# Layer normalisation without affine terms: the first tile loaded in halves and stored in parts, the last stores waited for on GpSimd

## The chip, the cores and the metric

The kernel runs on one core of a Trainium2 chip. The metric is the device time of one execution in microseconds (us). The profile is of one execution; its span reaches from the first to the last instruction of the program, and the device time is a little longer, since it takes in what lies around the program. The core has four engines that matter here: VectorE (DVE), ScalarE (ACT) and GpSimd (POOL) compute, SyncE (SP) only waits and starts transfers. Transfers between main memory (HBM) and on-chip memory run on 16 DMA engines, which take their work from queues; SP's transfers are on one queue (q1 in the profile), ACT's on another (q10).

## The reference

Each of the 32 x 512 = 16384 rows of 1024 floats is normalised on its own: its mean is taken off, and it is divided by the root of its variance plus eps.

```
def reference(x, eps):                     # x: (32, 512, 1024) float32
    mean = np.mean(x, axis=-1, keepdims=True)
    var = np.var(x, axis=-1, keepdims=True)
    return ((x - mean) / np.sqrt(var + eps)).astype(np.float32)
```

The input and the output are 67.11 MB each, so 134.2 MB have to be moved.

## The kernel before, in words

The 16384 rows are spread over the 128 partitions, which gives each partition 128 rows. They are cut into 17 tiles (line 10): 15 of 8 rows per partition, one of 6 and one of 2. A tile of 8 rows is 4096 KB; in main memory the rows of one partition lie side by side, so such a tile is moved as one contiguous run of 32 KB for each partition (`rows_of`, line 82).

On chip there is one buffer, `ring`, with room for 48 rows per partition, that is, for six tiles of 8 (lines 12 and 53). A tile is loaded into it, normalised in place and stored from it.

The order of the work is written out by hand; each engine has its own program, and they wait for each other through semaphores.

- SP issues all 17 loads (lines 93 to 104). The first six find room at once. Each later load waits until the stores of the tiles that had its rows before have landed (the semaphores `stored`, lines 100 and 104). So the load of tile 6 waits for the store of tile 0. `BESIDE` (line 16) could put loads on ACT's queue and is empty.
- DVE (`vector`, line 107) waits for a tile's load (`landed`), runs two `bn_stats` for each row, one for each half of the row's 1024 elements, and then a reciprocal, for which it waits for ACT's root.
- GpSimd (lines 145 to 190) merges the statistics of a tile in nine small operations, and makes the bias in a tenth, after the reciprocal.
- ACT (lines 193 to 213) takes the root for the tile, then normalises row after row with one ACTIVATE each (line 202), and issues the store of the whole tile (line 211), which waits until the tile's last row is done (`act`).
- At the end SP waits for the stores of the tiles that are still in the ring (lines 216 to 218). Then the engines meet in the program's closing: SP gives a signal (line 52 of the profile), each engine answers it, SP collects the answers, and GpSimd gathers all engines and clears the semaphores (line 249).

DVE's program for the middle tiles is a loop, which is why it compares with a value in a register there (lines 128 to 131). A DMA adds 16 to its semaphore when it has landed wholly, one for each DMA engine; `sixteens` (line 74) counts what a wait must reach.

Of the kernel before, what the change touches and what calls it, by code (L numbers as in the profile page):

```python
# [12 lines left out]

FIRST, TURNS = 3, 2

BESIDE = ()


@with_exitstack
def kernel(  # L20
# [6 lines left out]
    nc = tc.nc  # L27
# [3 lines left out]
    x2 = x.flatten_outer_dims()  # L31
    o2 = out.flatten_outer_dims()
# [10 lines left out]
    def sbuf(name, shape):  # L43
        return ctx.enter_context(nc.sbuf_tensor(name, shape, fdt))


    plan, row = [], 0
# [5 lines left out]
    ring = sbuf("ring", [P, SLOT * SLOTS, D])  # L53
# [13 lines left out]
    def places(name):  # L67
        out = [nc.alloc_semaphore(f"{name}_{t}") for t in range(FIRST + SLOTS)]
        for t in range(len(out), len(plan)):
            looped = t < FIRST + TURNS * SLOTS  # L70
            out.append(out[t - SLOTS] if looped else nc.alloc_semaphore(f"{name}_{t}"))
        return out

    def sixteens(sems, t):
        return 16 * sum(1 for s in sems[: t + 1] if s.num == sems[t].num)

    landed, rooted, stored = places("landed"), places("rooted"), places("stored")
    taken, inverse, pool, act = map(
        nc.alloc_semaphore, ("taken", "inverse", "pool", "act")
    )  # L80

    def rows_of(a, row, K):
        return a[row * P : (row + K) * P].rearrange("(p k) d -> p k d", p=P)

    def load(engine, t):
        K, row, at = plan[t]
        return engine.dma_start(  # L87
            out=ring[:, at : at + K, :], in_=rows_of(x2, row, K)
        ).then_inc(landed[t], 16)


    owner = {}
    for t, (K, row, at) in enumerate(plan):
        gone = sorted({owner[r] for r in range(at, at + K) if r in owner})
        owner.update((r, t) for r in range(at, at + K))
        if t in BESIDE:
            assert not gone
            load(nc.scalar, t)
            continue
        for g in gone[:-1]:  # L100
            nc.sync.wait_ge(stored[g], sixteens(stored, g))
        dma = load(nc.sync, t)
        if gone:
            dma._wait_ge(stored[gone[-1]], sixteens(stored, gone[-1]))


    def vector(t, arrived, turn):
        K, row, at = plan[t]
        for k in range(K):
            for s in range(NSUB):  # L110
                i = nc.vector.bn_stats(  # L111
                    out=stats[:, at + k, s, :],
                    in_=ring[:, at + k, s * BN_MAX : (s + 1) * BN_MAX],
                )
                if k == 0 and s == 0:
                    i._wait_ge(landed[t], arrived)
        i.then_inc(taken, 1)
        nc.vector.reciprocal(  # L118
            out=rstd[:, at : at + K], in_=std[:, at : at + K]
        )._wait_ge(rooted[t], turn).then_inc(inverse, 1)  # L120

    nc.vector.memset(eps_t[:], eps_val)  # L122
    for t in range(FIRST):
        vector(t, 16, 1)
# [3 lines left out]
    with nc.vector.Fori(16, 16 * TURNS + 1, 16) as arrived:  # L128
        for t in range(FIRST, FIRST + SLOTS):
            vector(t, nc.vector.lower_val(arrived), turn)  # L130
        nc.vector.reg_add(turn, turn, 1)
    for t in range(FIRST + TURNS * SLOTS, len(plan)):
        vector(t, 16, 1)
# [4 lines left out]
    def gp(i, sem, value):  # L138
        nonlocal npool
        i._wait_ge(sem, value).then_inc(pool, 1)  # L140
        npool += 1
        return pool, npool

    g = nc.gpsimd
    for t, (K, row, at) in enumerate(plan):
        parts = stats[:, at : at + K].rearrange("p g s (h c) -> p g (s h) c", h=2)
        mean4, m2 = parts[:, :, :, 1], parts[:, :, :, 2]
        nm, d, h = nmean[:, at : at + K], dev[:, :K], half[:, :K]
        n = gp(
            g.tensor_tensor(out=h, in0=mean4[:, :, 0:2], in1=mean4[:, :, 2:4], op=ALU.add),  # L150
            taken,
            t + 1,
        )
        n = gp(g.tensor_tensor(out=nm, in0=h[:, :, 0], in1=h[:, :, 1], op=ALU.add), *n)  # L154
        n = gp(
            g.tensor_scalar(out=nm, in0=nm, scalar1=-1.0 / H, scalar2=None, op0=ALU.mult),  # L156
            *n,
        )
        n = gp(
            g.tensor_tensor(  # L160
                out=d, in0=mean4, in1=nm.unsqueeze(2).to_broadcast([P, K, H]), op=ALU.add
            ),
            *n,
        )
        n = gp(g.tensor_mul(out=d, in0=d, in1=d), *n)  # L165
        n = gp(
            g.tensor_scalar(  # L167
                out=d, in0=d, scalar1=float(D // H), scalar2=None, op0=ALU.mult
            ),
            *n,  # L170
        )
        n = gp(g.tensor_tensor(out=d, in0=d, in1=m2, op=ALU.add), *n)  # L172
        n = gp(g.tensor_tensor(out=h, in0=d[:, :, 0:2], in1=d[:, :, 2:4], op=ALU.add), *n)  # L173
# [3 lines left out]
                    out=ss[:, at : at + K], in0=h[:, :, 0], in1=h[:, :, 1], op=ALU.add  # L177
# [7 lines left out]
                    out=nmr[:, at : at + K], in0=nm, in1=rstd[:, at : at + K]  # L185
# [7 lines left out]
    for t, (K, row, at) in enumerate(plan):  # L193
        nc.scalar.activation(  # L194
            out=std[:, at : at + K],
            in_=ss[:, at : at + K],
            func=AF.Sqrt,
            bias=eps_t[:],
            scale=1.0 / D,
        )._wait_ge(*summed[t]).then_inc(rooted[t], 1)  # L200
        for k in range(at, at + K):
            i = nc.scalar.activation(  # L202
                out=ring[:, k, :],
                in_=ring[:, k, :],
                func=AF.Identity,
                bias=nmr[:, k : k + 1],
                scale=rstd[:, k : k + 1],
            ).then_inc(act, 1)
            if k == at:
                i._wait_ge(*ready[t])  # L210
        nc.scalar.dma_start(
            out=rows_of(o2, row, K), in_=ring[:, at : at + K, :]
        )._wait_ge(act, row + K).then_inc(stored[t], 16)


    for t in range(len(plan)):
        if t in owner.values():
            nc.sync.wait_ge(stored[t], sixteens(stored, t))


# [33 lines left out]
```

## Time and profile before

| | us |
|---|---|
| time, median of 3 runs (lowest to highest) | 318.0 (317.92 to 318.02) |
| time of the profiled execution | 318.23 |
| its span | 316.6 |
| ACT: one row, line 202, mean of 128 | 1.227 |
| DVE: one half row, line 111, mean of 256 | 0.678 |
| load of 4096 KB, median from issue to landing | 43.9 |
| store of 4096 KB, median from issue to landing | 48.0 |
| first load, from issue to landing | 12.2 |

The time from issue to landing of a transfer holds the time that it waits behind others in its queue and shares the 16 DMA engines with the other queue; it isn't what the transfer would take alone. In the lines of the profile, a queue's instruction is marked by a q behind its engine's name (SPq, ACTq), and DMA shares and GB/s are means over the 16 DMA engines.

### The profile page before, as it was taken

The numbers are of one execution on the slowest core, as the hardware profiler recorded it, in microseconds if no ns is written. First come the engines' busy times: TensorE is split into PE (matmuls) and PEld (weight loads), VectorE is DVE, ScalarE is ACT, GpSimd is POOL, SyncE is SP. The second block draws the span as 40 slices with busy tenths as digits, with TensorE's granted clock in tenths as the row PEclk, the third lists the DMA queues.
The fourth block names the chain that finished last, engine by engine and source line by source line (L and its number), as shares of the span: only waits on it lengthen the run. The fifth ranks groups of instructions, "written<-read, shape, count | busy, mean of one in ns | idle before, by whom it ended". The sixth has DMA issues, their size and how long they took to land.

```text
span 316.6 us, 693 instructions
## 1 busy us (share of the span) xinstructions
DVE 156.8 (50%) x274; ACT 153.0 (48%) x146; POOL 39.3 (12%) x174
## 2 busy tenths in 40 slices
DVE  0387595875290743809347092561916519083000
ACT  1006595775915619074290833808347092567500
POOL 0002202112002020010201102020020200203100
DMA  8999999999999999999999999999999999999995
GB/s 331 397 464 402 426 431 397 461 402 460 423 440 439 422 451 410 455 410 451 410 460 414 447 418 435 418 443 431 439 443 418 447 418 435 431 431 422 455 421 254
DMA packets 4899, 134.24 MB, mean 424 GB/s; under 512 B 544, under 2 KB 544, under 8 KB 544
## 3 DMA queue, kind: packets, MB, share of 16 engines
q1 hardware_dynamic: 2448, 67.11, 49.6%
q10 hardware_dynamic: 2448, 67.11, 49.1%
q14 instruction: 3, 0.02, 0.0%
HBM read 67.11 MB, written 67.11 MB: 424 GB/s over the span
## 4 chain that ended last, share of the span: by engine, by line
DMA 54%; another core or an unknown queue 18%; ACT 9%; DVE 9%; POOL 2%; issue 1%; SPq 0%; ACTq 0%
DMA ring<-in_x_dram 31%; DMA out_dram<-ring 24%; ACT ring L202 9%; DVE stats L111 8%; ACT std L194 0%; SPq L87 0%; POOL dev L167 0%; POOL nmr L184 0%; DVE rstd L118 0%; POOL dev L172 0%; POOL nmean L156 0%; POOL dev L160 0%; POOL dev L165 0%; POOL half L150 0%
## 5 line engine op out<-in xcount | busy, mean ns | idle before, releaser
L111 DVE BATCH_NORM_STATS2 stats<-ring 128x6 f32<-128x512 f32 x256 | 153.5, 678 | 82.2 <-DMA ring<-in_x_dram 81.6
L202 ACT ACTIVATE ring<-ring,nmr,rstd 128x1024 f32<-128x1024 f32 x128 | 146.7, 1227 | 9.3 <-POOL nmr L184 9.3
L194 ACT ACTIVATE std<-ss,eps_t 128x8 f32<-128x8 f32 (+2 forms) x17 | 5.1, 300 | 134.7 <-POOL ss L176 134.3
L150 POOL TENSOR_TENSOR half<-stats 128x16 f32<-128x16 f32 (+2 forms) x17 | 3.9, 231 | 233.0 <-DVE stats L111 233.0
L118 DVE RECIPROCAL rstd<-std 128x8 f32<-128x8 f32 (+2 forms) x17 | 3.4, 200 | 55.4 <-ACT std L194 55.4
L167 POOL TENSOR_SCALAR dev<-dev 128x32 f32<-128x32 f32 (+2 forms) x17 | 5.0, 293 | 1.5
L184 POOL TENSOR_TENSOR nmr<-nmean,rstd 128x8 f32<-128x8 f32 (+2 forms) x17 | 3.5, 203 | 11.9 <-DVE rstd L118 11.9
L172 POOL TENSOR_TENSOR dev<-dev,stats 128x32 f32<-128x32 f32 (+2 forms) x17 | 4.3, 254 | 1.4
L160 POOL TENSOR_TENSOR dev<-stats,nmean 128x32 f32<-128x32 f32 (+2 forms) x17 | 4.1, 239 | 1.4
L165 POOL TENSOR_TENSOR dev<-dev 128x32 f32<-128x32 f32 (+2 forms) x17 | 4.0, 235 | 1.3
L156 POOL TENSOR_SCALAR nmean<-nmean 128x8 f32<-128x8 f32 (+2 forms) x17 | 4.0, 232 | 1.5
L173 POOL TENSOR_TENSOR half<-dev 128x16 f32<-128x16 f32 (+2 forms) x17 | 3.6, 213 | 1.3
L176 POOL TENSOR_TENSOR ss<-half 128x8 f32<-128x8 f32 (+2 forms) x17 | 3.4, 201 | 1.3
L154 POOL TENSOR_TENSOR nmean<-half 128x8 f32<-128x8 f32 (+2 forms) x17 | 3.4, 200 | 1.3
L194 ACT ACT_TABLE_LOAD x1 | 1.3, 1283 | 0.9 <-SPq L52 0.9
L122 DVE MEMSET eps_t<- 128x1 f32 x1 | 0.1, 59 | 1.0 <-SPq L52 1.0
L235 POOL MEMSET const-float32-0.0<- 128x1 f32 x1 | 0.1, 98 | 0.2 <-issue 0.2
L235 POOL MEMSET const-bfloat16-1.0<- 128x1 bf16 x1 | 0.1, 102 | 0.0
L235 POOL MEMSET const-uint8-127<- 128x1 uint8 x1 | 0.1, 101 | 0.0
L235 POOL MEMSET const-float32-1.0<- 128x1 f32 x1 | 0.1, 98 | 0.0
## 6 DMA issues: line engine op xcount, KB each, us to landing
ring<-in_x_dram SPq DMA_DIRECT2D x15, 4096.0 KB, 43.9
out_dram<-ring ACTq DMA_DIRECT2D x15, 4096.0 KB, 48.0
ring<-in_x_dram SPq DMA_DIRECT2D x1, 3072.0 KB, 41.4
out_dram<-ring ACTq DMA_DIRECT2D x1, 3072.0 KB, 18.3
ring<-in_x_dram SPq DMA_DIRECT2D x1, 1024.0 KB, 53.1
out_dram<-ring ACTq DMA_DIRECT2D x1, 1024.0 KB, 17.1
```

The source lines that it names most:

```text
L111: i = nc.vector.bn_stats(out=stats[:, at + k, s, :], in_=ring[:, at + k, s * BN_MAX : (s + 1) * BN_MAX],)
L118: nc.vector.reciprocal(out=rstd[:, at : at + K], in_=std[:, at : at + K])._wait_ge(rooted[t], turn).then_inc(inverse, 1)
L150: g.tensor_tensor(out=h, in0=mean4[:, :, 0:2], in1=mean4[:, :, 2:4], op=ALU.add),
L156: g.tensor_scalar(out=nm, in0=nm, scalar1=-1.0 / H, scalar2=None, op0=ALU.mult),
L160: g.tensor_tensor(out=d, in0=mean4, in1=nm.unsqueeze(2).to_broadcast([P, K, H]), op=ALU.add),
L165: n = gp(g.tensor_mul(out=d, in0=d, in1=d), *n)
L167: g.tensor_scalar(out=d, in0=d, scalar1=float(D // H), scalar2=None, op0=ALU.mult),
L172: n = gp(g.tensor_tensor(out=d, in0=d, in1=m2, op=ALU.add), *n)
L173: n = gp(g.tensor_tensor(out=h, in0=d[:, :, 0:2], in1=d[:, :, 2:4], op=ALU.add), *n)
L184: g.tensor_mul(out=nmr[:, at : at + K], in0=nm, in1=rstd[:, at : at + K]),
L194: nc.scalar.activation(out=std[:, at : at + K], in_=ss[:, at : at + K], func=AF.Sqrt, bias=eps_t[:], scale=1.0 / D,)._wait_ge(*summed[t]). ...
L202: i = nc.scalar.activation(out=ring[:, k, :], in_=ring[:, k, :], func=AF.Identity, bias=nmr[:, k : k + 1], scale=rstd[:, k : k + 1],).then ...
```

## The change

Four things change; the mathematics and the work of DVE and GpSimd on each tile stay as they are.

1. The first tile is loaded by two DMAs of 4 rows each. SP issues the first half, ACT the second, ahead of everything else on ACT. The second half has a semaphore of its own, `landed_later`, and DVE's first operation on row 4 of tile 0 waits for it.
2. The first tile's result is stored by three DMAs of 2, 2 and 4 rows, each issued by ACT as soon as its rows are normalised. `stored[0]` then counts to 48 before the load of tile 6 may go.
3. GpSimd, and not SP, waits for the last stores.
4. `BESIDE` and the function `load` go; the loop over the other loads stays on SP.

```diff
-BESIDE = ()
+HALVES, PARTS = (4, 4), (2, 2, 4)
...
     def sixteens(sems, t):
+        if sems is stored and t == 0:
+            return 16 * len(PARTS)
         return 16 * sum(1 for s in sems[: t + 1] if s.num == sems[t].num)
...
+    later = nc.alloc_semaphore("landed_later")
+    K, row, at = plan[0]
+    first = 0
+    for n, engine, sem in zip(HALVES, (nc.sync, nc.scalar), (landed[0], later)):
+        engine.dma_start(
+            out=ring[:, at + first : at + first + n, :],
+            in_=rows_of(x2, row, K)[:, first : first + n, :],
+        ).then_inc(sem, 16)
+        first += n
+    assert first == K
+    owner = {r: 0 for r in range(K)}
+    for t, (K, row, at) in list(enumerate(plan))[1:]:
...
                 if k == 0 and s == 0:
                     i._wait_ge(landed[t], arrived)
+                if t == 0 and k == HALVES[0] and s == 0:
+                    i._wait_ge(later, 16)
...
+        parts = PARTS if t == 0 else (K,)
+        ends = [sum(parts[: i + 1]) for i in range(len(parts))]
         for k in range(at, at + K):
             i = nc.scalar.activation(
...
-        nc.scalar.dma_start(
-            out=rows_of(o2, row, K), in_=ring[:, at : at + K, :]
-        )._wait_ge(act, row + K).then_inc(stored[t], 16)
+            if k - at + 1 in ends:
+                n = parts[ends.index(k - at + 1)]
+                a = k + 1 - n
+                nc.scalar.dma_start(
+                    out=rows_of(o2, row, K)[:, a - at : a - at + n, :], in_=ring[:, a : a + n, :]
+                )._wait_ge(act, row + k - at + 1).then_inc(stored[t], 16)
 
 
     for t in range(len(plan)):
         if t in owner.values():
-            nc.sync.wait_ge(stored[t], sixteens(stored, t))
+            nc.gpsimd.wait_ge(stored[t], sixteens(stored, t))
```

In main memory a partition's 8 rows stay side by side; a half takes 16 KB out of each run of 32 KB, and the parts take 8, 8 and 16 KB.

More of the change, by code (lines that the diff above doesn't have):

```diff
@@ L83, in rows_of @@
         return a[row * P : (row + K) * P].rearrange("(p k) d -> p k d", p=P)
-    def load(engine, t):
-        K, row, at = plan[t]
-        return engine.dma_start(
+    later = nc.alloc_semaphore("landed_later")
[10 more added lines that the diff above has]
+    for t, (K, row, at) in list(enumerate(plan))[1:]:
+        gone = sorted({owner[r] for r in range(at, at + K) if r in owner})
+        owner.update((r, t) for r in range(at, at + K))
+        for g in gone[:-1]:
+            nc.sync.wait_ge(stored[g], sixteens(stored, g))
+        dma = nc.sync.dma_start(
             out=ring[:, at : at + K, :], in_=rows_of(x2, row, K)
         ).then_inc(landed[t], 16)
[L92 to L102, printed above, removed]
         if gone:
```

## The prediction

> **What bounds the kernel now.** I read the page's slices first, then its queue lines, then the table of stretches, and only then the chain of waits, because the chain is made of transfers and says little about what a transfer is worth. From the page:
>
> ```profile
> span 316.6 us, 693 instructions
> DVE 156.8 (50%) x274; ACT 153.0 (48%) x146; POOL 39.3 (12%) x174
> DMA  8999999999999999999999999999999999999995
> q1 hardware_dynamic: 2448, 67.11, 49.6%
> q10 hardware_dynamic: 2448, 67.11, 49.1%
> ```
>
> No compute engine is busy for more than half the span, while the 16 DMA engines are at nine tenths or more in all slices but the first and the last. The queues (q1 the loads, q10 the stores) together fill 98.7% of the engines' time. The stretches (us, DVE, ACT, POOL busy, clock, DMA share, GB/s) show that it is full whatever the mix:
>
> ```profile
> 0.00:2.00 2.00, 0.06 (x1) 1.11 (x1) 0.19 (x4) 1.00 0.18 49
> 2.00:4.00 2.00, 0.00 (x0) 0.17 (x1) 0.00 (x0) 1.00 0.96 328
> 12.00:36.00 24.00, 19.25 (x33) 9.46 (x9) 2.58 (x12) 1.00 1.01 437
> 36.00:42.00 6.00, 3.19 (x7) 2.98 (x4) 2.06 (x9) 1.00 0.93 350
> 60.00:160.00 100.00, 51.24 (x90) 52.39 (x52) 13.93 (x60) 1.00 1.01 435
> 288.00:308.00 20.00, 2.64 (x5) 9.07 (x9) 2.07 (x10) 1.00 1.01 436
> 312.00:314.00 2.00, 0.00 (x0) 0.00 (x0) 0.00 (x0) 1.00 0.86 365
> 314.00:316.60 2.60, 0.00 (x0) 0.00 (x0) 0.00 (x0) 1.00 0.02 6
> ```
>
> Loads alone (12 to 36) move 437 GB/s, loads and stores 435, stores alone (288 to 308) 436. So a store that starts earlier only takes the place of a load, and the end stays at 134.24 MB / 435 GB/s = 308.6 us of transfers plus what is lost at the edges: 1.9 us before the first packet, a slow first round of packets, the dip at 36 to 42, an uneven finish, and the closing of the program. The beginning, end and the first store in the timeline and the chain:
>
> ```profile
> 0.93 2.92 SPq L87 DMA_DIRECT2D ring<-in_x_dram  x6
> 0.93 12.16 DMA ring<-in_x_dram
> 35.64 0.37 ACTq L211 DMA_DIRECT2D out_dram<-ring  x1
> 35.64 25.00 DMA out_dram<-ring
> 38.47 0.30 ACT L194 ACTIVATE std<-ss,eps_t 128x8 f32<-128x8 f32 x1 [2.87 <-POOL ss L176]
> 298.02 0.34 ACTq L211 DMA_DIRECT2D out_dram<-ring  x1
> L218 SPq EVENT_SEMAPHORE  x3: 28/28/28, 305.5 to 315.2; - x3
> ```
>
> The last store is issued at 298.0 but its last share lands only at 315.16 (the event that ends L218's wait): 17 us of stores lie queued ahead of it, so the compute of the last tiles is not on the path either.
>
> **What the Trainium skill says.** DMA: Bandwidth & Descriptors, Where 436 GB/s comes from, puts the ceiling of the 16 engines at 435 GB/s; the stretches agree. Its section Issuing engines are not separate DMA queues says that transfers started by several engines share the same 16 and that only issue time is saved; the equal 437 and 435 with one and two queues agree. Queues, rings and completion order has each DMA engine take turns between its queues by packet. The packet records agree: between 276 and 287 us the last load's 8 KB packets hold 3.2 engines and the 32 KB stores beside them 12.8, one to four, as in turns of one packet each. Latency and other measured facts gives 207 GB/s against 214 at a 512 KiB row pitch; here the parts are 8 and 16 KB at a 32 KB pitch, which nothing before shows.
>
> **The change, part by part.**
>
> *Smaller packets.* A packet of 32 KB takes 1213 ns, one of 24 KB 912, one of 8 KB 309 (medians of the packet records; the six-row and two-row tiles have the latter). The slope is (1213 - 309) / 24 = 37.7 ns per KB, which leaves 309 - 8 x 37.7 = 7.7 ns per packet. Each engine carries 8 packets of the first load and 8 of its store now; in halves of 16 KB the load has 16, and in parts of 8, 8 and 16 KB the store has 24. That is 24 more, 24 x 7.7 = 0.18 us, and three more completion packets of 9 ns: **+0.21 us** on every DMA engine, on the bound with nothing to hide it.
>
> *The wait moved to GpSimd.* The records of the end: SP sees the last share at 315.18, passes the two other waits and a branch, and signals at 315.40; the other four report back, and SP reads their signals one by one until 315.68, drains at 315.73 and 315.80, and GpSimd's collecting wait passes at 315.83. When GpSimd waits, SP has signalled long before and the others' reports lie there. GpSimd goes 315.18, branch, its own report at about 315.44 (its branch at the start took 0.17 us to the next instruction against SP's 0.12), SP's last read at 315.49 and drains until 315.60, GpSimd at 315.63. **-0.20 us**. GpSimd has nothing behind this wait but its part of the closing, and SP's loads are all issued by 236 us, so the wait's move blocks no work. If GpSimd wakes slower than I take it, the gain is 0; below -0.3 it can't go, since the 0.29 us of SP's reading is all there is to remove.
>
> *Halves on both queues.* Both halves are issued at about 0.9 us (SP's first issue is at 0.93, ACT's table load, whose place the new issue takes, at 0.89). They alternate on the same engines, so both land near 13.1, the first one packet (0.6 us) earlier at best. DVE may begin that much earlier, off the path. The table load moves 0.5 us later and is needed at 25.6. The first packets start between 1.93 and 3.00 us and the early ones take up to 2.2 us instead of 1.21, so that all engines finish their first at about 4.0. I take the same with two queues: 0, between -0.5 (each queue feeds the engines in half the time) and +1.06 (the two take turns and the spread of 1.06 us doubles).
>
> *Parts of the first store.* Two more issues on ACT: at the end of the run, an issue between two ACTIVATEs costs 294.43 to 294.82, 0.4 us, so 0.8 us in tile 0. ACT then is idle for 2.87 us before 38.47, which covers it; uncovered it would move tile 1's store by 0.8, with DMA still full. The first part is ready after two of eight rows, 26.44 + 2 x 1.15 + about 0.1 = 28.8 instead of 35.6. Its 8 KB packets alternate with 32 KB loads, so it gets a fifth: 1.05 MB / 87 GB/s = 12 us, the second the same, the third (16 KB, a third) 2.1 MB / 145 = 14.5. With the 4.0 us that the first store needed from issue to its first packet (packet records, 39.67), the parts end at 45, 57 and 71: the *whole* tile is stored later than now (60.64). The load of tile 6 waits for that and goes at about 71 instead of 60.65. Meanwhile loads get four fifths, so the six loaded ahead finish near 69 to 74 instead of 3.36 + 81.8 = 85.1. For up to 3 us the load queue may be empty. Stores of tiles 1 and 2 (issued at 48.5 and 61.4, 8.4 MB or 19 us of transfers) lie queued and cover it: 0. Without that cover it would be those 3 us and 1.0 us until a new load's packets. Afterwards loads run about one tile further ahead than now, so the tail keeps its backlog.
>
> Sum: +0.21 - 0.20 + 0 = 0. The profiled execution took 318.23 us, 316.6 of span and 1.6 around it; it lies 0.2 above the median of 318.0, and the edit changes it by 0.01. I say **318.0**; by its own unknowns (tail 0 to -0.3, issue within half a microsecond) 317.5 to 318.6.
>
> **Rivals.** *Faster, the dip goes.* In 36 to 42 us the loads' packets are slow just as the store queue is used for the first time; their excess over 1213 ns sums to 12 us, 0.75 per engine. If it is the price of waking ACT's queue, the half load pays it under the slow first round. 318.0 - 0.75 = 317.2. For: time and place. Against: ten loads' packets at 193 to 196 us are slow too, with no queue new, so it may be memory alone; and it may come with the first store all the same.
>
> *Slower, the start on two queues.* If descriptors for the two issues are made in turn, the last DMA engine begins 1.06 us later. Every engine has the same bytes and none ever waits, so a late beginner ends late: the last store's shares land between 313.88 and 315.16. That decides once the last engine's start slips by over 0.65 us; the time is 318.0 + 1.06 = 319.1. For: the spread at the start shows that making descriptors takes time. Against: SP's six issues, 0.37 to 0.51 us each, show no stall of that size, and packets are half as long. The unseen pitch works the same way: 3% (207 against 214) of 8.4 MB, 19.3 us, is 0.6.
>
> *Nothing reaches the end but the tail*: packets cost less than I sum, 317.8, inside no change.
>
> **How the numbers follow.** Forecast 0.56, the dip's going 0.23 (with a better spread at the start), late start or pitch 0.21. The measurement tells from no change what is over 0.2%, 0.64 us. The range runs from 317.1 to 319.0, which takes in the faster case and most of the slower.
>
> **What would show it.** Right: 435 GB/s from 12 to 36; the three parts landing near 45, 57 and 71; tile 6 loaded from 71; SP's closing 0.2 us shorter after the last landing. Wrong: a stretch after 70 us below 430 GB/s (the cover failed), first packets starting after 3.0 us, or no dip at the first store.

## The result and the profile after

The changed kernel takes 320.39 us (median of 4 runs, 319.77 to 320.61) against 318.0: 1.0073 times as long, with a 95% interval from 1.0055 to 1.009. The forecast of 318.0 was wrong, and the time lies outside its range.

| | before | after |
|---|---|---|
| profiled execution, its span | 318.23, 316.6 | 320.49, 318.7 |
| landing of the last store's 16 shares, first to last | 313.88 to 315.16 | 313.57 to 317.43 |
| from the last landing to the end of the span | 1.46 | 1.24 |
| device time less the moment of the last landing | 3.07 | 3.06 |
| issue of the first store (part) | 35.64 | 29.34 |
| landing of the whole first tile's store | 60.64 | 72.09 |
| issue of tile 6's load | 60.65 | 72.10 |

(Landings and issues, here and below, are the trace's semaphore and instruction records.) From the page of the changed kernel, the busy engines, the slices and the queues:

```profile
span 318.7 us, 696 instructions
DVE 156.5 (49%) x274; ACT 153.3 (48%) x146; POOL 39.3 (12%) x174
DMA  7999999999999999999999999999999999999994
q10 hardware_dynamic: 2880, 69.21, 50.8%
q1 hardware_dynamic: 2448, 65.01, 47.6%
```

The DMA engines are still busy in all slices but the first and last, and DVE, ACT and POOL do what they did. So the page shows no new idle time. The table of stretches of the changed kernel (columns as in the prediction):

```profile
0.00:2.00 2.00, 0.06 (x1) 0.69 (x1) 0.19 (x4) 1.00 0.20 41
2.00:4.00 2.00, 0.00 (x0) 0.60 (x1) 0.00 (x0) 1.00 0.91 303
12.00:36.00 24.00, 19.17 (x33) 8.52 (x9) 2.32 (x10) 1.00 1.00 430
36.00:42.00 6.00, 2.78 (x7) 3.64 (x5) 2.32 (x10) 1.00 1.00 431
60.00:160.00 100.00, 53.89 (x96) 57.97 (x56) 13.93 (x60) 1.00 1.01 430
288.00:308.00 20.00, 0.17 (x1) 3.84 (x5) 0.64 (x4) 1.00 0.98 423
312.00:314.00 2.00, 0.00 (x0) 0.00 (x0) 0.00 (x0) 1.00 0.74 315
314.00:316.00 2.00, 0.00 (x0) 0.00 (x0) 0.00 (x0) 1.00 0.31 131
316.00:318.70 2.70, 0.00 (x0) 0.00 (x0) 0.00 (x0) 1.00 0.04 18
```

Two things are to be seen. The dip of before at 36 to 42 us (350 GB/s) is gone. And the end is ragged: in 312 to 314 us only 74% of the DMA engines' time is used, in 314 to 316 only 31%, where before there was 2% left after 314. So the loss isn't in transfers waiting for compute. Some of the 16 engines finish over 3 us after the others, and each of them has the same bytes to move.

Where they fell behind is in the packet records. The trace doesn't number the DMA engines, but packets follow each other on one without a gap, so they can be strung together. Two kinds of string from 70 us on in the changed kernel (L a load packet, S a store packet of 32 KB, in us and ns; l and s the packet that completes a DMA):

```
11 engines   ... L 69.36+1213  S(16 KB) 70.58+611  l  s  S 71.19+1213  S 72.40+1213  S 73.61+1213  S 74.82+1213  L 76.03+1213 ...
 5 engines   ... l 70.58  S(16 KB) 70.58+611  s  S 71.19+1213  S 72.40+1213  S 73.61+1213  S 74.82+1880  S 76.71+2458  L 79.17+1213 ...
```

The load queue is empty from 71 us, because tile 6's load waits until 72.10. When it comes back, five engines stall for (1880 - 1213) + (2458 - 1213) = 1.9 us (1.8 to 2.3) in two store packets. More slow packets follow around 87 us. The stretch from 71 to 79 us, of the kernel before and then of the changed one, shows what this looks like in a mean:

```profile
71.00:79.00 8.00, 4.57 (x9) 4.26 (x5) 2.25 (x10) 1.00 1.06 459
71.00:79.00 8.00, 4.78 (x10) 4.77 (x5) 2.17 (x10) 1.00 1.06 426
```

The DMA share is the same, and 33 GB/s less pass: a stalled packet counts as busy. Over 8 us that is 0.26 MB, which at 435 GB/s takes 0.6 us, as five engines of 16 stalled for 1.9 us do (an estimate from these figures). The sign of being wrong that the prediction named, a stretch after 70 us below 430 GB/s, has come, though it is a weak one by itself, since the kernel before has 421 from 79 to 84 us. The experiments ask why these five.

### The profile page after: what moved, and what is told of

It is laid out like the page before. It is cut to its first block, busy times and chain, and to the rows that moved or that the text cites. A ratio compares the mean times of both kernels' runs of the same rounds, so it can differ in the third digit from the quotient of the medians.

```text
span 318.7 us, 696 instructions
## 1 busy us (share of the span) xinstructions
DVE 156.5 (49%) x274; ACT 153.3 (48%) x146; POOL 39.3 (12%) x174
## 4 chain that ended last, share of the span: by engine, by line
another core or an unknown queue 42%; DMA 27%; DVE 12%; ACT 6%; POOL 3%; issue 1%; SPq 1%; ACTq 0%
DMA out_dram<-ring 15%; DMA ring<-in_x_dram 12%; DVE stats L115 11%; ACT ring L210 6%; SPq L104 1%; ACT std L200 0%; POOL dev L173 0%; POOL dev L178 0%; DVE rstd L124 0%; POOL dev L166 0%; POOL nmean L162 0%; POOL dev L171 0%; POOL half L156 0%; POOL half L179 0%
```

## The experiments

"The kernel before" of each comparison was run on the same chip beside it. The first four divide the change, and test the empty load queue by itself.

**e1_gpsimd_only**

```diff
-            nc.sync.wait_ge(stored[t], sixteens(stored, t))
+            nc.gpsimd.wait_ge(stored[t], sixteens(stored, t))
```

> The kernel before with the last stores waited for on GpSimd and nothing else changed. My theory of the changed kernel (A): its load queue ran empty at 71 us, since the load of tile 6 had to wait for the last part of the first store, and when that load came in at 75 us five of the sixteen DMA engines stalled for about 1.8 us and never made it up. This edit doesn't touch that, so A expects only the shorter closing: 0.2 us less than the kernel before, 317.8. Rival B, that the wait's move costs the time (GpSimd wakes late), expects 320. The time between the last landing and the end of the span should be 1.2 us instead of 1.46 in both cases of A.

317.86 beside 317.95, ratio 0.9997 (0.9989 to 1.0006). From the last landing to the end of the span it is 1.24 us instead of 1.46, as expected. But the time outside the span is 1.8 us (317.74 - 315.9) instead of 1.6: in all runs it is 1.8 to 2.0 where GpSimd waits, and 1.6 where SP does. From the last landing to the end of the device time it is 3.06 us here and was 3.07 before. So the wait's move costs nothing, and what it gains within the span doesn't reach the device time.

**e2_no_parts**, from the changed kernel

```diff
-HALVES, PARTS = (4, 4), (2, 2, 4)
+HALVES, PARTS = (4, 4), (8,)
```

> The changed kernel, but with the first tile's result stored by one DMA of 8 rows: halves of the load and GpSimd's wait stay. A: tile 0 is stored by about 60 us, the load of tile 6 goes at 60 us while the load queue still has over 20 us of work, no engine falls behind, the last store's shares land within 1.5 us of each other: 317.8 (0.2 from the closing, 0.1 for the halves' packets back, perhaps 0.7 less if the dip at the first store is gone). Rival C, that the two-queue start puts the engines out of step: 320, with the spread of landings at the end near 4 us.

317.86 beside 317.95, 0.9997 (0.9987 to 1.0007). The last shares land within 0.95 us. The two-queue start as such puts no engine 3 us behind. The dip at the first store stayed (0.7 us per engine in slow packets from 35 to 40 us), though ACT's queue had been used at 0.9 us: my rival that this was the price of waking that queue falls.

**e3_parts_44**, from the changed kernel

```diff
-HALVES, PARTS = (4, 4), (2, 2, 4)
+HALVES, PARTS = (4, 4), (4, 4)
```

> The changed kernel with the first store in parts of 4 and 4 rows. Its packets of 16 KB get a third of the engines beside loads, so by my sum the tile is stored at about 64 us and the six first loads end near 72: the load queue has 4 us or more left when the load of tile 6 is issued, about what a new load needs until its first packet (3.8 us). A: no stall or a small one, 317.8 to 318.3. Rival D, that storing in parts costs in itself, by small packets beside large ones or by more DMAs on ACT: 319.5 or more, as in the changed kernel.

317.89 beside 317.95, 0.9996 (0.9988 to 1.0004). Tile 0 was stored at 66.6 us, and the sixth load ended at 79: the queue didn't run empty. Parts and more DMAs on ACT cost nothing that can be measured.

**e4_dry_before**, from the kernel before

```diff
+        if t == SLOTS:
+            nc.sync.wait_ge(taken, SLOTS)
         dma = load(nc.sync, t)
```

> The kernel before, with one more wait: the load of tile 6 goes only when VectorE has finished tile 5, about 95 us instead of 60.65. No halves, no parts. The load queue is then empty from 85 us to about 99, while the store queue has work for all of that time. A: the engines stall as the loads come back, some of them more than others, and fall out of step: 319 to 321, the last store's shares landing over 3 us apart. Rival D (parts and small packets are to blame): 318.0, since the DMA engines have stores to carry while the loads are away.

321.85, 1.0135 (1.0116 to 1.0154): slower, as theory A expected, by a little more than its 319 to 321 and for another reason. Not one packet is slow when the loads come back at 99 us, and the last store's shares land within 0.2 us of each other. The stretches of this run:

```profile
84.00:100.00 16.00, 9.79 (x17) 6.09 (x7) 2.32 (x10) 1.00 0.99 429
100.00:288.00 188.00, 88.14 (x153) 86.42 (x84) 20.90 (x90) 1.00 1.00 433
288.00:300.00 12.00, 7.62 (x14) 7.07 (x7) 2.19 (x10) 1.00 0.91 391
300.00:312.00 12.00, 2.30 (x5) 9.56 (x9) 2.14 (x11) 1.00 0.79 339
```

While the load queue was empty (84 to 100) the DMA engines were full; the loss is after 288, where the last tiles' compute is waited for, since the loads had lost their lead over the stores. So an empty load queue stalls nothing by itself, and my theory A falls.

The second four: is it repeatable, is it a meeting in time, is it the empty queue?

**f1_after_again**: no edit.

> The changed kernel unchanged, for a second profile. If the stall is the kernel's own, packets of the store queue over 1.7 us appear again on several DMA engines around 75 to 79 us and the last store's shares land over 3 us apart. If it was chance (memory), the slow packets lie elsewhere or are gone.

319.63 in its one run. Slow store packets again at 75 to 76 us, this time on 9 engines, and slow load packets at 85 to 87 on most. It is the kernel's own.

**f2_after_delayed**, from the changed kernel

```diff
+        if t == SLOTS:
+            nc.sync.wait_ge(act, 33)
         dma = nc.sync.dma_start(
```

> The changed kernel, with the load of tile 6 held back until ACT has done one row of tile 4, about 80 us instead of 72. The load queue is empty all the longer (71 to 84 us), the store queue still full. The kernel before with an empty load queue from 85 to 99 us showed no stall at all, so the empty queue alone isn't it. Theory A2: what stalls is the meeting of two things, ACT's issue of the next store (75.50) within the 4 us in which the first packets of a load come into an empty queue. Here the load comes in from 80 to 84, between ACT's issues at 75.5 and 88.4: A2 expects no packet over 1.7 us between 70 and 95 us, shares of the last store within 1.5 us, 318. Theory A3, that the first store's small parts leave the engines in unlike order and so stall some of them at any restart: slow packets at 80 to 87 us and 320.

319.13 in its one run. Slow packets at 83.5 to 86 us on 7 engines. The stall moved with the load's coming back, away from ACT's issues: A2 falls.

**f3_dry_meets_issue**, from the kernel before: as e4_dry_before, with `nc.sync.wait_ge(act, 37)` for the wait.

> The kernel before, with the load of tile 6 held back until ACT has done five of eight rows of tile 4: issued at about 85 us, when the load queue has just run empty (85.3), its first packets due near 89, and ACT's issue of tile 4's store between the two, at 88.4. No halves, no parts. A2: several engines stall between 88 and 93 us and end late, 319.5 to 321. A3 (parts): no stall, 318.

318.49 beside 317.92, 1.0026 (1.0003 to 1.0048), but single runs from 317.62 to 321.98. No stall at 88 to 93 us, against A2; in the profiled run, of 320.38, a few packets were slow near every end of a load instead. Inconclusive.

**f4_early_refill**, from the changed kernel

```diff
-FIRST, TURNS = 3, 2
+FIRST, TURNS = 7, 1
...
+        if t == SLOTS:
+            first = 0
+            for n, sem, gate in zip(PARTS, refilled + [landed[t]], part_stored):
+                nc.sync.dma_start(
+                    out=ring[:, at + first : at + first + n, :],
+                    in_=rows_of(x2, row, K)[:, first : first + n, :],
+                ).then_inc(sem, 16)._wait_ge(gate, 16)
+                first += n
+            continue
...
```

The parts of the first store have semaphores of their own here, and DVE waits for each part of tile 6.

> The changed kernel with halves, parts of 2, 2 and 4 and GpSimd's wait all kept, but the load of tile 6 cut in the same parts, each of which waits only for the part of the first store that had its rows (VectorE's loop covers six tiles once instead of twice, so that tile 6 can have its own waits). The first refill is issued at about 46 us, so the load queue never runs empty. A and A2: no stall, 317.8 to 318.2 (two more DMAs and small packets cost 0.1 to 0.2). A3 in the form that parts alone do it: 319.5 or more.

322.32, 1.0125 (1.0099 to 1.0151), single runs from 321.62 to 326.81: slower than the changed kernel, with the load queue never empty. Some 20 packets took over 1.3 us near each end of a load from 90 us on, which lay 0.7 to 1.8 us from an end of a store. So an empty queue isn't needed for a loss either. From this came theory H, that two ends lying close stall an engine.

**g1_late_root** and **g2_late_two**, from the kernel before: tile 0's store is moved behind the root of tile 1, and behind two rows of tile 1. (Parts of both edits; the comments say whose a line is, and `store` is a function that holds the lines taken out.)

```diff
...
         )._wait_ge(*summed[t]).then_inc(rooted[t], 1)
+        if t == 1:                    # g1_late_root
+            store(0)
...
+            if t == 1 and k == at + 1:    # g2_late_two
+                store(0)
-        nc.scalar.dma_start(
-            out=rows_of(o2, row, K), in_=ring[:, at : at + K, :]
-        )._wait_ge(act, row + K).then_inc(stored[t], 16)
+        if t > 0:
+            store(t)
```

> The kernel before, with nothing changed but the place of the first tile's store in ACT's program: after the root of tile 1, so it is issued at 38.8 us instead of 35.6. The same transfers and sizes, no parts, no halves, the load queue not empty. Theory H, from the landings of the earlier runs: a DMA engine that comes to the end of a load and of a store within some 4 us stalls, now and again, and the engines drift apart. In the kernel before each load ends 5.7 us after a store, and no packets are slow there; where the two ends lie 1 us apart (early refill) some 20 packets are slow at every one. A delay of the first store by d moves the two ends towards each other by about 2d (the store ends d later; the loads, alone for d longer, end d earlier), so 3.2 us bring 5.7 to about 0.7. H: slow packets at nearly every end of a load from 80 us on, the last store's shares over 3 us apart, 320 to 322. Theory A3 (the small parts do it) and A (the empty queue): 318.0.

> As g1_late_root, but the first store goes after two rows of tile 1, at about 41.7 us: 6 us late, twice as late as there. H: the ends then lie about 6.4 us apart the other way round (the store after the load), no packets are slow, 318.0. If it is the delay of the first store as such that costs, this one costs more than g1_late_root.

g1: the ends (medians over the engines) lay within 0.03 us of each other from 61 us on, closer than aimed at, and hardly a packet was slow at any of them: eleven took over 1.3 us after 60 us. It took 318.85, 1.0027 (1.001 to 1.0043). In the profiled execution (319.08) one engine lost 1.6 us in one load packet at the first store (2836 ns at 41.6 us); its share of the last store landed at 316.01, the others' by 314.55. g2: 333.64, 1.0492 (1.0464 to 1.0521). The first store went at 39.4 us, not 41.7, since ACT's queue issues it while a row is still running; the ends lay 2.4 us apart, some 30 packets took over 1.3 us at most of them, and two of the last store's 16 shares landed at 332.2 us, the other fourteen by 320.0. What delays these two is open. H, that closeness decides, falls with g1; the sensitivity to the moment of the first store is larger than anything I had thought of.

**g3_parts_only**, from the kernel before

```diff
+        parts = PARTS if t == 0 else (K,)
+        ends = [sum(parts[: i + 1]) for i in range(len(parts))]
...
+            if k - at + 1 in ends:
+                n = parts[ends.index(k - at + 1)]
+                a = k + 1 - n
+                nc.scalar.dma_start(
...
```

> The kernel before with the first store in parts of 2, 2 and 4 rows, and no other part of the change: one whole load, SP waits at the end. All theories that put the loss down to the parts (by way of the late store of tile 0 and the load that comes in at 75 us) expect the changed kernel's time plus the closing's 0.2: 320 to 320.6. If the halves have a share in it, less.

317.89 beside 317.89, 0.9995 (0.9982 to 1.0008), against every theory so far. The load queue ran empty here too (tile 0 stored at 72.87, tile 6's load issued at 72.88), and nothing stalled.

**g4_restart_mid**, from the changed kernel: as f2_after_delayed, with `nc.sync.wait_ge(act, 31)`.

> The changed kernel with halves, parts and GpSimd's wait, and the load of tile 6 held back by 2 us more, until ACT has done seven rows of tile 3: issued at about 74.3, first packets at about 78. In the changed kernel they come at 75.9, 4 us after a store ended and the next began (72); when I held the load back to 80 they came at 84.4, 3.6 us after the next store's end (80.7). Here they fall in the middle, 6 us from either. The load queue is empty longer than in the changed kernel. H: no packet over 1.7 us from 74 to 90 us, the last store's shares within 1.5 us, 317.7 to 318.2. A3: 319.1 to 320.5, as in the two runs with parts and an empty queue.

320.14, 1.0066 (1.0043 to 1.0089): five engines stalled at 76 to 79 us. H falls here too.

The strings of packets of g3_parts_only and the changed kernel differ 40 us earlier, where the first store part comes in (S' a store packet of 8 KB; three engines of each kind, from about 28 us):

```
g3_parts_only   28.15 LLLlLS'LS'LS'    28.26 LLLlLS'LS'LS'    28.53 LLLlLS'LS'LS'     (all 16 but the last engine or two)
after           28.08 LLLlLS'LS'LS'    28.16 LLLlLS'LS'LS'    28.30 LLLlLS'LS'LS'     (11 engines: first S' from 33.04 to 33.66)
after           28.07 LLLlLLS'LS'LS'   28.14 LLLlLLS'LS'LS'   28.28 LLLlLLS'LS'LS'    (5 engines: first S' from 34.15 to 34.37)
```

Five engines missed the turn and took one load packet more. They are the five strings that end in "l S s" at 70 us: their loads run one turn ahead of the others', so on them the last load packet comes before the store's last packet, and not after it. These are also the strings that stall: they start four S packets one after the other from 71.08 to 71.45 us on, and the fourth, at 74.71 to 75.07, is the first slow one. The part went out at 29.34 us instead of 28.92, since with halves the first tile's SP half lands at 13.59 instead of 13.18. So the halves may matter only by the moment. Five runs move the moment by an ACTIVATE into a spare tile between rows 0 and 1 of tile 0 (i1 and i2 by two):

```diff
             if k == at:
                 i._wait_ge(*ready[t])
+            if t == 0 and k == 0:
+                nc.scalar.activation(
+                    out=spare[:], in_=ring[:, 2, :800], func=AF.Identity
+                )
...
```

**h1_after_pause**: the changed kernel, 800 columns.

> The changed kernel, whole, with one more ACTIVATE (128 x 800, into a spare tile) between the first two rows of tile 0, so the first store part is issued about 0.9 us later, at 30.25 us instead of 29.34. Theory O: what matters is the order in which each DMA engine takes turns between the queues. In the changed kernel's profile the first store packets come in at about 33.0 us, just as the engines end a load packet (32.93 to 33.7): 5 engines missed the turn and took one load packet more than the other 11 before their first store packet. Those 5 run one turn apart from the rest from then on, and it is 5 engines that stall when the load queue comes back at 75 us and end late. In the run of the parts alone all engines but one took the same turn, and nothing stalled. 0.9 us later, at about 33.9, all 16 engines are inside the same packet: O expects one order on all of them, no packet over 1.7 us around 75 to 90 us, the last store's shares within 1.5 us, 317.6 to 318.1. Theory A3 (halves and parts and the empty queue together cost): 320, since all three are kept.

318.95 beside 317.94, 1.0033 (1.0023 to 1.0042). The pause was 0.76 us, but SP's half had landed earlier and the part moved only to 29.88. 12 engines were late and 12 stalled.

**h2_parts_pause**: parts only, 500 columns.

> The kernel before with the first store in parts alone (which took no more time than before), with one more ACTIVATE (128 x 500) between the first two rows of tile 0: the first part is issued at about 29.5 us instead of 28.92. There the engines end a load packet between 33.0 and 33.4 us (two later), and the first store packets came in before that, at about 32.6. 0.6 us later they come in at 33.2, in the middle of these ends. O: some engines take the store packet one turn earlier than others, slow packets when the load queue comes back at about 76 us, the last store's shares over 3 us apart, 319 to 321. All that puts the loss down to the halves of the first load: 317.9.

319.05, 1.0039 (1.0027 to 1.0051): as expected, 7 engines late, 7 stalled at 75 to 78 us. From the timeline of ACT in g3_parts_only and then in this run:

```profile
26.52 2.37 ACT L206 ACTIVATE ring<-ring,nmr,rstd 128x1024 f32<-128x1024 f32 x2 [0.56 <-POOL nmr L186]
28.92 0.38 ACTq L218 DMA_DIRECT2D out_dram<-ring  x1
```

```profile
26.54 1.24 ACT L207 ACTIVATE ring<-ring,nmr,rstd 128x1024 f32<-128x1024 f32 x1 [0.55 <-POOL nmr L187]
27.69 0.60 ACT L217 ACTIVATE spare<-ring 128x500 f32<-128x500 f32 x1
28.20 1.23 ACT L207 ACTIVATE ring<-ring,nmr,rstd 128x1024 f32<-128x1024 f32 x1
29.45 0.37 ACTq L223 DMA_DIRECT2D out_dram<-ring  x1
```

All that the edit moves is the issue of the first store's three parts, each 0.53 us later (the second at 32.28 instead of 31.75, the third at 37.33 instead of 36.80); tile 1's store goes at 48.62 and 48.61.

**h3_parts_gpsimd**: parts only, and GpSimd's wait as in e1.

> The kernel before with the first store in parts of 2, 2 and 4 and GpSimd's wait, without the halves. The parts alone took 317.89 beside 317.89 and GpSimd's wait alone 317.86 beside 317.95; the closing is 0.2 us shorter with it. If the two add up: 317.7.

317.61 beside 317.94, 0.9993 (0.9978 to 1.0009), single runs from 317.38 to 320.26. Its median is 0.3 us below before, but the interval doesn't tell it from no change, and one of its 14 executions, of 320.26, has the changed kernel's time. The wait on GpSimd has no part in the 0.3 (see e1_gpsimd_only).

**i1_after_pause2** and **i2_parts_pause2**: the changed kernel with 800 and 370 columns, parts only with 800 and 480.

> The changed kernel, whole, with a longer pause between the first two rows of tile 0 (ACTIVATEs of 128 x 800 and 128 x 370 into a spare tile). The pause before moved the first store part only to 29.88 us, and its packets, due near 33.5, still met the ends of load packets (33.0 to 33.6): 4 engines took them one turn earlier than the other 12, and it took 318.95. Now the part should be issued at about 30.3 and its packets come in at 33.9, after the last of these ends and before the next (34.15). O: one order on all 16 engines, at most stray slow packets from 74 to 90 us, 317.6 to 318.1. If halves and parts together cost whatever the moment: 319 or more.

> The parts alone, with a pause of 1.25 us (128 x 800 and 128 x 480): the first part issued at about 30.15 us, its packets due near 33.8. At 28.92 it cost nothing (317.89, one order), at 29.45 it cost 1.1 us (319.05, 7 engines against 9). O: one order again, on the other side, and 317.7 to 318.1 although it is later still. If a later first part costs as such: over 319.05.

318.9, 1.0039 (1.0025 to 1.0052), and 319.02, 1.0036 (1.0022 to 1.005). In both, all 16 engines were late (in i1 four of them by two turns), and O, which had called one order free, was wrong: nearly all stalled, each for less. The stretches of g3_parts_only and then of i2_parts_pause2:

```profile
71.00:79.00 8.00, 4.77 (x10) 4.57 (x6) 2.34 (x10) 1.00 1.04 449
79.00:84.00 5.00, 5.00 (x10) 5.00 (x5) 0.00 (x0) 1.00 0.98 421
84.00:90.00 6.00, 3.95 (x7) 3.98 (x4) 1.47 (x7) 1.00 1.01 437
```

```profile
71.00:79.00 8.00, 4.78 (x10) 4.58 (x6) 2.32 (x10) 1.00 1.00 403
79.00:84.00 5.00, 5.00 (x9) 5.00 (x5) 0.00 (x0) 1.00 0.99 428
84.00:90.00 6.00, 3.86 (x7) 3.88 (x4) 1.56 (x7) 1.00 1.00 388
```

The DMA share is full in both (1.00 and more), and yet 403 GB/s pass instead of 449, and 388 instead of 437: once more, a stalled packet counts as a busy engine. In i2, slow packets sum to 0.57 us per engine from 75 to 80 us and 0.56 from 85 to 90, which is the 1.1 us lost.

**j1_parts_pause0**: parts only, 190 columns.

> The parts alone with a pause of only 0.25 us (128 x 190): the first part issued at about 29.17 us. In the run with a pause of 1.25 us all 16 engines took the first store packet one turn late, in one order, and still all of them stalled, so unlike orders aren't the cause by themselves. Theory O2: an engine that takes its first store packet one turn late stalls when the load queue comes back at 75 us; the fewer they are, the longer each stalls and the later it ends, since the others don't wait for it (5 late engines: 320.1 and 320.3; 7: 319.05; 12: 318.95; 16: 319.0; none: 317.6 and 317.9). At 29.17 a few engines, 2 to 6, should be late. O2: as many stall, and it takes 319.3 to 320.5, the changed kernel's time without its halves. If the halves cost something of their own, it stays under 319.

319.39 beside 317.77, 1.0055 (1.0035 to 1.0074), with single runs from 317.47 to 320.95. Here the profiled execution was the fastest of all: the part went at 28.99, no engine was late, nothing stalled, 317.47. So the forecast of 2 to 6 late engines missed in this execution. Others of the same program took up to 320.95, 3.5 us more, so a loss as large as the changed kernel's comes without halves; how many engines were late in them isn't recorded. The moment does differ from execution to execution: in four of them, after, f1, f2 and g4, whose programs are the same up to the first part, it was issued at 29.34, 29.40, 29.30 and 29.05 us, with 5, 9, 7 and 5 late engines.

All profiled executions with parts of 2, 2 and 4 and an empty load queue, by the count of late engines (first store packet at 34.15 us or later, when those on time start before 33.7):

| run | first part issued | late engines | engines or packets stalled as loads come back | its time |
|---|---|---|---|---|
| j1, h3, g3 | 28.99, 28.89, 28.92 | 0, 0, 0 | none | 317.47, 317.87, 318.07 |
| after | 29.34 | 5 | 5 engines, twice each | 320.49 |
| g4 | 29.05 | 5 | 5 engines, twice each | 321.53 |
| f2 | 29.30 | 7 | 7 | 319.13 |
| h2 | 29.45 | 7 | 7, one twice | 319.05 |
| f1 | 29.40 | 9 | 9 | 319.63 |
| h1 | 29.88 | 12 | 12, packets over 1.4 us | 318.59 |
| i1, i2 | 30.36, 30.14 | 16, 16 | 11 and 15 packets over 1.5 us | 318.72, 318.87 |

No late engine, no stall; as many late, about as many stalled. Followed packet by packet from the first store to the stall, the late engines and the stalled ones are the same in g4, h1 and h2. With five late engines each loses 1.8 to 2.3 us as the loads come back; with all late (i2) they lose 0.57 on the mean there and 1.1 in all.

But a missed turn and an empty queue aren't enough either. In e4_dry_before 12 engines took one load packet more than the other 4 before their first store packet (41.02 us or later, the others by 40.02), in f3_dry_meets_issue 10 more than the other 6; the load queue ran empty in both (16 and 6 us lie between the starts of two load packets), and no engine stalled when it came back. There the first store went whole. So the table holds for parts of 2, 2 and 4, and what they add isn't shown.

## Why the prediction was wrong

The step that failed is in *Parts of the first store*: "For up to 3 us the load queue may be empty. Stores of tiles 1 and 2 ... lie queued and cover it: 0." The facts in it were right: the parts landed at 45.7, 58.5 and 72.1 us (45, 57 and 71 forecast), tile 6's load went at 72.10 (71), the queue was empty, and the stores kept all DMA engines busy. What I priced at 0 was the queue's coming back. It cost 1.8 to 2.3 us on five engines, with more at the next ends of transfers, so that the last share landed at 317.43 instead of 315.16 us: 2.27 us, the whole loss of the profiled execution (320.49 against 318.23). With this first store, the engines that had let its first packet pass by one turn paid it; the counts of eleven profiled executions agree with this, and none had the one without the other. Why such an engine stalls, what it waits for in those 1.9 us, no run shows. It stays open; unlike orders among the engines (i2), the empty queue alone (e4 and g3), a missed turn together with an empty queue (e4, f3) and the closeness of ends (g1, g4) are ruled out as the whole reason.

The sum was made as if 16 DMA engines were one. That the last of them sets the end I had used, but only for the start, in the slower rival: its mechanism (a DMA engine that falls behind ends late, and nobody waits for it) is what happened, at 75 us, not at 2 us, with another cause. First packets started between 1.92 and 2.73 us, no later than before. Nor does anything show of the 0.6 us estimated for the unseen pitch: packets of 8 and 16 KB took 309 and 611 ns, on the slope of the others.

*Halves on both queues*: 0 was right as a direct cost (e2), and the Trainium skill's sentence that issuing on several engines only saves issue time (DMA: Bandwidth & Descriptors, Issuing engines are not separate DMA queues) agrees. But "the first one packet earlier at best" was the wrong way round. ACT's packet went first on every engine, SP's half, for which DVE waits, landed last, and DVE began at 13.61 instead of 13.11. Off the path, as I said; but those 0.5 us moved the first store part into the ends of the load packets. That this is all the halves do is likely, since h2 and j1 lose without them, but not shown: no two runs have the same moment with and without halves.

*Smaller packets*: a 16 KB packet took 611 ns, as the slope says. The 0.21 us can't be seen by itself; e3 and g3, which have most of it, took no longer than before.

*The wait on GpSimd*: within the span -0.22 us (1.24 after the last landing instead of 1.46), against a forecast of -0.20. But the sum took 1.6 us around the span as fixed, and that became 1.8 (320.49 - 318.7). In the device time the term is 0: 3.06 us after the last landing instead of 3.07.

*Faster rival*: the dip at the first store did go, one of the signs against the forecast: the excess of slow packets sums to 0.01 us per engine from 35 to 42 us, against 0.76 before. But from 42 to 70 us it sums to 0.43, against 0.03, so about half of it came back. In g3, which has neither the dip nor the stall, the last share landed at 315.00 us, against 315.16 in the kernel before, and the time is 317.89 beside 317.89: the dip's going was worth nothing that can be measured. It isn't ACT's queue being woken (e2 keeps the dip). It goes when the first store comes in small parts, for g3 hasn't got it either. Why is open.

## What to carry to other kernels

Where transfers are the bound, look at the landing of each share of the last store, not at the DMA share of the page: a stalled packet counts as busy, and the slowest of 16 engines sets the end. That another queue covers an empty one doesn't make it free; here its coming back cost nothing in some kernels (e4, g3) and 2 us on some engines in others, and only a run told which. Cutting a transfer into smaller packets can make a queue run empty, since beside large packets small ones get the smaller share (the first tile was stored at 72.09 us instead of 60.64). When a time depends on how two streams meet, shift the moment by a few tenths of a microsecond before believing in any single cause, and look at the spread of the executions. And a gain read from the end of the span has to be looked for in the device time too.

## What the runs showed of the hardware that I had not expected

- A transfer on an empty queue, beside a full one, shows its first packets 3.7 to 4.0 us after its issue (29.34 to 33.04, 72.10 to 75.94, in the kernel before 35.64 to 39.67), in which an engine moves about three packets of the other queue at 1.21 us each. On idle DMA engines it was 1.0 us (0.93 to 1.93).
- Issuing the three parts of one tile's store 0.53 us later cost 1.1 us in 317.9 (h2), and one 4 MB store 3.8 us later cost 15.7 us (g2), with the same bytes in the same sizes.
- The two queues take turns packet by packet, whatever the sizes (L S' L S' with 32 KB and 8 KB), as the Trainium skill has it (DMA: Bandwidth & Descriptors, Queues, rings and completion order). A turn that is missed as the second queue starts is kept: in the changed kernel from 34 to 70 us.
- Which engine waits for the last stores moves 0.2 us between the end of the span and the time around it: 1.46 and 1.6 us with SP (before), 1.24 and 1.8 with GpSimd (e1).
